# Moving the tiles of a decoder layer to other addresses in SBUF

## The chip, the cores and the metric

The kernel runs on one core of one Trainium2 chip. The metric is the device time of one execution in microseconds. One execution of the kernel before was also profiled; its span, from the first to the last instruction, is a little shorter than the time measured for that execution.

## The reference

One layer of a hybrid decoder on 256 tokens of width 2048, all in float32. A normalised input goes through one wide projection into the queries, keys and values of two attention branches (8 heads of 128 each), 8 forget logits and two gates. The branches are merged through sigmoid gates, projected and added to the input. Then comes an MLP of width 8192 with a squared ReLU, and a last normalisation.

```python
hn = rms_norm(x, norm_mix_g)
z = hn @ w_in                                   # 2048 -> 6*1024 + 8 + 2*2048
a   = merge_heads(moba_attention(...)) @ w_proj_a
bfx = merge_heads(forgetting_attention(...)) @ w_proj_b
merged = sigmoid(g_a) * a + sigmoid(g_b) * bfx
x = x + merged @ w_out                          # 2048 -> 2048
hm = rms_norm(x, norm_mlp_g)
x = x + square(relu(hm @ w_up)) @ w_down        # 2048 -> 8192 -> 2048
out = rms_norm(x, norm_final_g)
```

With 256 tokens there is a single block of MoBA, so that branch is plain causal attention with ALiBi.

## The kernel before

**Weights.** All weights come from HBM in chunks of 1 MB (`load`, line 92), each into one of three `raw` tiles of 128 partitions by 8 KB. Every float32 number is used as a sum of two float32r parts, high and low. ScalarE writes the high part of a piece of a chunk into a slot of the ring `his` (12 slots, line 135, `emit_high`), and VectorE subtracts it from the chunk and writes the low part into the ring `los` (10 slots, line 150, `emit_low`). A slot has 512 float32 columns, which are 2 KB in each partition. A chunk of kind "W" also has four sums of its blocks in the tile `sum` (lines 162 to 164), which are split in the same way: with them a product of 2x2 blocks takes seven multiplications in place of eight.

**Activations.** The factors of a large product (the transposed input, and blocks and sums of blocks of it) are split in the same way and lie in the one tile `big`, 2 x 52 factors of 128 columns (512 bytes) each. The tiles named `pr` (pool `pair`, nine buffers of 4 KB) hold split activations of the plain products, head pairs, merged rows and MLP rows. `row` tiles (three of 8 KB) hold results of a group of columns, `tmp` tiles (five of 2 KB) short-lived rows.

**Products.** Every large product is the function `triple` (line 326): three matmuls into one PSUM bank, high x high, high x low, low x high. The factor is the stationary operand (128 x 128), the split weight the moving one (512 columns; 256 in one short stretch at the end). There are 5604 of these matmuls, nearly all of TensorE's work. Between them stand small blocks into the bank `aux`: transposes (lines 684, 644, 753: moving operand `ident`), scores and values of attention (609, 610, 658, 659) and the forget logits (537, 539).

**Order.** The order on every engine is fixed in the program. `pump` issues splits as slots of the rings come free, `boundary` puts small tasks between pieces of the large products. The DMA of chunk q+3 is issued on SP's queue when VectorE has finished with chunk q. ScalarE's queue issues six DMAs; GpSimd issues none.

**Addresses.** A tile's address in its partition follows from the order of allocation. At the start of SBUF lies a reserve for dynamic DMAs (16 KB by default), then four small constants, and then the pools in turn: `const` (with `his`, `los` and small tables), `big`, `pair`, `rows`, `wraw`, `work`. Whatever is added at the front shifts all that follows.

Of the kernel before, what the change touches and what calls it, by code (L numbers as in the profile page):

```python
# [7 lines left out]
FT = mybir.dt.float32  # L8
# [54 lines left out]
def hybrid_layer(ctx: ExitStack, tc, x, xt, gcols, w_in, w_f, b_forget, w_proj_a, w_proj_b, w_out,  # L63
                 w_up, w_down, norm_final_g, out):
    nc = tc.nc
    const = ctx.enter_context(tc.tile_pool(name="const", bufs=1))
# [10 lines left out]
    chunks = []  # L77
    raw = {}
    split = {}
    his = const.tile([128, HI_SLOTS, 512], FR, name="his")  # L80
    los = const.tile([128, LO_SLOTS, 512], FR, name="los")

# [615 lines left out]
            del state["qk", h]  # L698


    acc2 = const.tile([128, NT, 4], FT, name="acc2")
    inv2 = const.tile([128, NT], FT, name="inv2")
    acc3 = const.tile([128, NT, 5], FT, name="acc3")
# [286 lines left out]
```

## Time and profile before

| | |
|---|---|
| time, median of 3 runs (lowest, highest) | 1362.66 us (1362.04, 1363.45) |
| the profiled execution, its own time | 1362.37 us |
| its span | 1360.7 us |
| TensorE matmul busy | 1342.2 us (99%) |
| TensorE weight load busy | 1108.5 us (81%) |
| VectorE busy | 1076.9 us (79%) |
| ScalarE busy | 797.4 us (59%) |
| GpSimd busy | 20.3 us (1%) |
| DMA engines, mean rate | 193 GB/s |

The matmuls overlap in the pipeline, so a matmul's listed duration is longer than its distance to the next one; the distance between two starts is what a matmul costs in a row of them. A span of many matmuls divided by their number gives it directly. Weight loads lie beside the matmuls. The other engines are bounds only in a stretch where they are busy nearly all the time.

### The profile page before, as it was taken

What the parts mean: (1) busy time and instruction counts of PE and PEld (TensorE: products, weight loads), DVE (VectorE), ACT (ScalarE), POOL (GpSimd) and SP (SyncE); (2) the same over time, 40 slices, a digit from 0 to 9 for tenths busy, and PEclk for the clock granted to TensorE, in tenths of its full rate; (3) what the DMA queues carried; (4) which work ended last, traced back from release to release, by engine and by line L of the source; (5) the groups of instructions that cost most, each with busy time, mean ns of one, the idle gap of its engine ahead of it and who ended that gap; (6) DMA issues with size and microseconds to landing.
All of it is one profiled execution on the core that took longest, in us unless ns stands there. A gap on an engine that the chain in (4) does not pass through costs nothing.

```text
span 1360.7 us, 16488 instructions
## 1 busy us (share of the span) xinstructions
PE 1342.2 (99%) x6132; PEld 1108.5 (81%) x6132; DVE 1076.9 (79%) x1319; ACT 797.4 (59%) x1033; POOL 20.3 (1%) x29
## 2 busy tenths in 40 slices
PE   9999999999999999999999999999999999999997
PEld 7778888877788888888788888888888888888886
DVE  5789999999977996666899557995579955799664
ACT  6766677766664565555566544665446653467532
POOL 0000000012100000000000000000000000000000
PEclk9999999999999999999999999999999999999999
DMA  8555555445465566564466654565645665556661
GB/s 311 186 185 187 186 186 186 157 155 184 160 211 186 188 211 222 175 243 169 157 216 223 205 189 165 189 234 188 201 168 186 221 212 186 183 188 216 225 203 69
DMA packets 93824, 262.25 MB, mean 193 GB/s; under 512 B 4656, under 2 KB 5040, under 8 KB 93104
## 3 DMA queue, kind: packets, MB, share of 16 engines
q1 hardware_dynamic: 92752, 257.97, 55.4%
q10 hardware_dynamic: 992, 3.24, 0.6%
q8 instruction: 48, 0.79, 0.2%
q14 instruction: 32, 0.26, 0.1%
HBM read 259.09 MB, written 2.10 MB: 192 GB/s over the span
## 4 chain that ended last, share of the span: by engine, by line
PE 89%; DVE 6%; ACT 3%; issue 1%; DMA 1%; POOL 0%; SPq 0%; POOLq 0%; ACTq 0%; DVEq 0%
PE P L326 85%; DVE los L150 2%; PE aux L684 2%; DMA raw<-in_w_in_dram 1%; ACT his L135 1%; DVE sum L162 1%; DVE sum L163 0%; PE aux L658 0%; PE aux L610 0%; PE aux L644 0%; ACT row L713 0%; ACT pr L460 0%; ACT big L418 0%; ACT row L486 0%; PE aux L753 0%
## 5 line engine op out<-in xcount | busy, mean ns | idle before, releaser
L326 PE MATMUL P<-his,big 128*128 128x512 f32 x2152 | 693.3, 396 | 0.5 <-ACT row L392 0.5
L135 ACT ACTIVATE his<-raw 128x1024 fp32r<-128x1024 f32 (+1 forms) x494 | 474.4, 970 | 361.9 <-PE P L326 347.6
L150 DVE TENSOR_TENSOR los<-raw,his 128x1024 fp32r<-128x1024 f32 (+1 forms) x511 | 537.3, 1080 | 141.2 <-PE P L326 99.4
L326 PE MATMUL P<-his,pr 128*128 128x512 f32 (+1 forms) x1584 | 491.1, 388 | 1.8 <-ACT his L501 1.8
L326 PEld LDWEIGHTS P<-his,big 128*128 128x128 f32 x2152 | 405.3, 188 | 85.8 <-ACT row L392 1.3
L326 PE MATMUL P<-los,big 128*128 128x512 f32 x1076 | 420.1, 390 | 0.0
L326 PEld LDWEIGHTS P<-his,pr 128*128 128x128 f32 x1584 | 295.9, 188 | 60.8 <-ACT his L501 2.1
L326 PE MATMUL P<-los,pr 128*128 128x512 f32 (+1 forms) x792 | 305.7, 386 | 0.0
L326 PEld LDWEIGHTS P<-los,big 128*128 128x128 f32 x1076 | 203.0, 189 | 40.1
L150 DVE TENSOR_TENSOR los<-sum,his 128x1024 fp32r<-128x1024 f32 (+1 forms) x158 | 163.9, 1073 | 12.2 <-PE P L326 11.0
L326 PEld LDWEIGHTS P<-los,pr 128*128 128x128 f32 x792 | 149.1, 188 | 29.2 <-DVE los L502 0.4
L135 ACT ACTIVATE his<-sum 128x1024 fp32r<-128x1024 f32 (+1 forms) x148 | 142.8, 982 | 31.6 <-PE P L326 18.9
L162 DVE TENSOR_TENSOR sum<-raw 128x1024 f32<-128x1024 f32 x68 | 82.9, 1220 | 0.9 <-DMA raw<-in_w_in_dram 0.9
L164 DVE TENSOR_TENSOR sum<-sum,raw 128x512 f32<-128x512 f32 x68 | 47.5, 698 | 2.3
L163 DVE TENSOR_TENSOR sum<-sum,raw 128x512 f32<-128x512 f32 x68 | 47.5, 698 | 2.3
L772 DVE TENSOR_TENSOR pr<-tmp,pr 128x512 fp32r<-128x512 f32 x32 | 22.0, 689 | 30.0 <-ACT pr L771 30.0
L684 PEld LDWEIGHTS aux<-ident,row 128*128 128x128 f32 x224 | 27.9, 142 | 9.1 <-DVE cumT L591 1.3
L684 PE MATMUL aux<-ident,row 128*128 128x128 f32 x224 | 33.6, 272 | 1.2 <-DVE cumT L591 0.9
L769 ACT ACTIVATE tmp<-aux 128x512 f32<-128x512 f32 x32 | 19.1, 598 | 26.2 <-PE aux L684 26.1
L407 DVE TENSOR_TENSOR big<-pr,big 128x384 fp32r<-128x384 f32 (+1 forms) x16 | 10.0, 624 | 23.4 <-ACT big L406 23.4
L631 ACT ACTIVATE tmp<-tmp,stat 128x128 f32<-128x128 f32 (+1 forms) x32 | 14.3, 447 | 16.9 <-DVE stat L623 16.8
L776 DVE SCALAR_TENSOR_TENSOR row<-P,inv,row 128x512 f32<-128x512 f32 x24 | 17.1, 749 | 8.9 <-PE P L326 8.9
(138 smaller groups left out, 513.4 us busy)
## 6 DMA issues: line engine op xcount, KB each, us to landing
raw<-in_w_in_dram SPq DMA_DIRECT2D x79, 1024.0 KB, 5.3
raw<-in_w_up_dram SPq DMA_DIRECT2D x64, 1024.0 KB, 5.0
raw<-in_w_down_dram SPq DMA_DIRECT2D x64, 1024.0 KB, 5.2
raw<-in_w_out_dram SPq DMA_DIRECT2D x16, 1024.0 KB, 5.1
raw<-in_w_proj_a_dram SPq DMA_DIRECT2D x8, 1024.0 KB, 5.2
raw<-in_w_proj_b_dram SPq DMA_DIRECT2D x8, 1024.0 KB, 5.2
row<-in_xt_dram SPq DMA_DIRECT2D x8, 256.0 KB, 8.3
row<-in_x_dram SPq DMA_DIRECT2D x2, 1024.0 KB, 7.5
```

The costliest lines, as they stand in the source:

```text
L135: nc.scalar.activation(his[:, s:s + m], src[:, j:j + m], AF.Copy)
L150: nc.vector.tensor_tensor(los[:, s + jj:s + jj + mm], src[:, j + jj:j + jj + mm], his[:, h:h + mm].bitcast(FT), OP.subtract)
L162: nc.vector.tensor_tensor(t[:, 0:2], r[:, 1:3], r[:, 0:1].to_broadcast([128, 2, 512]), OP.add)
L163: nc.vector.tensor_tensor(t[:, 2], t[:, 0], r[:, 2], OP.add)
L164: nc.vector.tensor_tensor(t[:, 3], t[:, 2], r[:, 3], OP.add)
L326: nc.tensor.matmul(p, l, r[:, :n], start=first and j == 0, stop=last and j == 2)
L407: nc.vector.tensor_tensor(fa[:, 1, o + i:o + 4], f[:, i:4], fa[:, 0, o + i:o + 4].bitcast(FT), OP.subtract)
L631: nc.scalar.activation(t[:, sl], t[:, sl], AF.Exp, bias=st[:, tok:tok + 1], accum_out=st[:, 2 + tok:3 + tok])
L684: nc.tensor.transpose(p[:, c, s * 128:(s + 1) * 128], src[:, tok, (i + c) * 128:(i + c + 1) * 128], ident)
L769: nc.scalar.activation(t, p, AF.Square)
L772: nc.vector.tensor_tensor(h[:, :, 1], t, h[:, :, 0].bitcast(FT), OP.subtract)
L776: nc.vector.scalar_tensor_tensor(t, p, inv2[:, tok:tok + 1], t, op0=OP.mult, op1=OP.add)
```

## The change

The reserve for dynamic DMAs is set to 1 KB, and two unused tiles of 960 bytes are allocated: one ahead of `his`, one ahead of the last small tables of the pool `const`. No instruction is added, removed or moved on any engine, and no wait differs: only line numbers and addresses do.

```diff
+    const.tile([128, 240], FT, name="pad")
     his = const.tile([128, HI_SLOTS, 512], FR, name="his")
     los = const.tile([128, LO_SLOTS, 512], FR, name="los")
...
+    const.tile([128, 240], FT, name="pad2")
     acc2 = const.tile([128, NT, 4], FT, name="acc2")
...
-    nc = _bacc.Bacc("TRN2", target_bir_lowering=False, num_devices=1)
+    nc = _bacc.Bacc("TRN2", target_bir_lowering=False, num_devices=1, dynamic_dma_scratch_size=1024)
```

In the two programs as built, the addresses in bytes from the start of a partition are:

| tile | before | mod 2048 | mod 128 | after | mod 2048 | mod 128 |
|---|---|---|---|---|---|---|
| `his` (moving operand) | 16512 | 128 | 0 | 2112 | 64 | 64 |
| `los` (moving operand) | 41088 | 128 | 0 | 26688 | 64 | 64 |
| `ident` (moving operand of transposes) | 61792 | 352 | 96 | 47392 | 288 | 32 |
| `big` (stationary operand) | 68736 | 1152 | 0 | 55296 | 0 | 0 |
| `pr`, first of nine (stationary operand) | 121984 | 1152 | 0 | 108544 | 0 | 0 |
| `row`, first of three | 158848 | 1152 | 0 | 145408 | 0 | 0 |
| `raw`, first of three (written by DMA) | 183424 | 1152 | 0 | 169984 | 0 | 0 |
| `tmp`, first of five | 208000 | 1152 | 0 | 194560 | 0 | 0 |
| `sum` | 218240 | 1152 | 0 | 204800 | 0 | 0 |

Since slots are 2 KB and factors 512 bytes long, before the change the moving and the stationary operand of every large matmul begin at the same place within 512 bytes (128); after it the moving operand begins 64 bytes after the place of the stationary one.

## Rows read from the trace of the kernel before

**Rows 1.** The page: busy time of each engine, and slices of DVE.

```profile
PE 1342.2 (99%) x6132; PEld 1108.5 (81%) x6132; DVE 1076.9 (79%) x1319; ACT 797.4 (59%) x1033; POOL 20.3 (1%) x29
...
DVE  5789999999977996666899557995579955799664
```

**Rows 2.** Chain that ended last, longest pieces: start us, us, what.

```profile
381.58 162.62 PE P L326 x717
...
763.54 119.05 PE P L326 x525
```

**Rows 3.** Busy time by stretch: stretch, its length, each engine, PEclk, DMA share, GB/s.

```profile
70.00:140.00 70.00, 68.77 (x313) 55.99 (x312) 62.84 (x71) 47.23 (x59) 0.00 (x0) 0.98 0.56 190
140.00:270.00 130.00, 129.12 (x610) 106.99 (x609) 125.54 (x178) 92.19 (x144) 0.00 (x0) 1.00 0.51 175
270.00:420.00 150.00, 148.27 (x668) 119.18 (x667) 133.06 (x187) 98.17 (x157) 14.90 (x8) 1.00 0.54 183
420.00:700.00 280.00, 278.89 (x1261) 230.76 (x1260) 220.71 (x261) 159.31 (x203) 0.00 (x0) 1.00 0.58 197
...
71.00:72.30 1.30, 1.30 (x4) 0.99 (x3) 0.30 (x1) 1.30 (x2) 0.00 (x0) 0.50 0.41 63
```

**Rows 4.** The same for line 326 alone (PE, PEld, clock, DMA, GB/s).

```profile
270.00:420.00 150.00, 137.53 (x568) 104.80 (x567) 1.00 0.54 183
420.00:700.00 280.00, 275.62 (x1197) 223.35 (x1196) 1.00 0.58 197
700.00:1000.00 300.00, 296.92 (x1291) 240.91 (x1290) 1.00 0.58 198
1000.00:1360.00 360.00, 349.24 (x1566) 285.99 (x1564) 1.00 0.55 187
```

**Rows 5.** Timeline of TensorE while half the clock was granted: start us, us, what.

```profile
71.09 0.63 PE L326 MATMUL P<-los,big 128*128 128x512 f32 x1
71.52 1.05 PE L326 MATMUL P<-his,big 128*128 128x512 f32 x2
72.37 0.63 PE L326 MATMUL P<-los,big 128*128 128x512 f32 x1
```

**Rows 6.** Chain from 380 us: float32 matmuls of 256 columns, two records each.

```profile
380.27 0.43 PE aux L658 x2
```

**Rows 7.** Groups of TensorE's matmuls: line, operands, shapes, count, busy us, mean ns.

```profile
L684 PE MATMUL aux<-ident,row 128*128 128x128 f32 x224 | 33.6, 272 | 1.2 <-DVE cumT L591 0.9 <-ACT cum L583 0.4
...
L609 PE MATMUL aux<-pr 128*128 128x128 f32 x32 | 6.2, 275 | 0.9 <-ACT tmp L646 0.9
```

**Rows 8.** Groups of VectorE, then of ScalarE, same columns.

```profile
L150 DVE TENSOR_TENSOR los<-raw,his 128x1024 fp32r<-128x1024 f32 x377 | 457.2, 1221 | 137.4 <-PE P L326 96.4 <-issue 21.8 <-ACT his L135 16.4
...
L150 DVE TENSOR_TENSOR los<-raw,his 128x512 fp32r<-128x512 f32 x134 | 87.9, 685 | 3.7 <-PE P L326 3.0 <-ACT his L135 0.4
...
L163 DVE TENSOR_TENSOR sum<-sum,raw 128x512 f32<-128x512 f32 x68 | 47.5, 698 | 2.3
L135 ACT ACTIVATE his<-raw 128x1024 fp32r<-128x1024 f32 x394 | 414.0, 1057 | 332.7 <-PE P L326 323.7 <-DMA raw<-in_w_in_dram 2.2 <-DMA raw<-in_w_out_dram 2.0
...
L135 ACT ACTIVATE his<-raw 128x512 fp32r<-128x512 f32 x100 | 62.0, 626 | 29.2 <-PE P L326 24.0 <-DMA raw<-in_w_in_dram 3.5 <-DMA raw<-in_w_up_dram 1.7
```

**Rows 9.** DMA: queues by kind, and waits of SP's queue (us, times, longest).

```profile
q1 hardware_dynamic: 92752, 257.97, 55.4%
q10 hardware_dynamic: 992, 3.24, 0.6%
...
SPq L92 <- DVE los L150: 1142.6, 228, 15.5
```

**Rows 10.** Chain at the program's start: start us, us, what.

```profile
1.72 5.04 DMA raw<-in_w_in_dram
...
7.14 9.54 DMA raw<-in_w_in_dram
```

## The prediction

> **What bounds the kernel now.** I read the page's busy times first, then the chain of waits, then the table by stretch, then the distance between matmuls. TensorE is busy 99% of the span [rows 1], and the chain of waits runs through line 326 in pieces of hundreds of matmuls without another engine between them [rows 2]. So the time is the number of matmuls times the distance between two of them, and the question is whether addresses set that distance. 162.62 us over 717 matmuls are 226.8 ns, and 119.05 over 525, the first of three such pieces, are 226.8 again [rows 2]. These pieces use all slots of `his` and `los` and both `big` and `pr`.
>
> 512 columns at the granted 2.4 GHz are 213.3 ns, so each matmul has 13.5 ns on top. While half the clock was granted, as from 71.0 to 72.3 us [rows 3], the starts stand at 71.09, 71.52 and, two matmuls later, 72.37 us [rows 5]: three matmuls in 1.28 us, 426.7 ns each, which is 512 columns at 1.2 GHz with nothing on top. So the 13.5 ns belong to something that the slower array hides: the supply of operands, or a fixed pause between two matmuls. This is the only thing that I see on the path that an address could change. Float32 matmuls of 256 columns, each in two records, take 0.43 us for two records, 215 ns each [rows 6]: the same 213.3 ns of array time with only 2 ns on top. There columns are taken at half the rate, so again there is slack in the supply.
>
> VectorE is the second bound, and only early: 125.54 of 130 us between 140 and 270 us, 133.06 of 150 after that, 220.71 of 280 from 420 on [rows 3], as its row of slices also shows [rows 1]. The DMA queue is no bound: SP's queue stood 1142.6 us waiting for VectorE to give a `raw` tile back [rows 9].
>
> **The change part by part.** No instruction, order or wait differs. All that can change is how long something takes.
>
> *Moving operands, from 0 to 64 bytes past a multiple of 128.* 5508 matmuls of 512 columns (the 5604 of line 326 less 96 of 256) begin elsewhere. Every large matmul before has the same place within 128 bytes, so no row shows line 326 at another one; it has to be bounded. From below: the 215 ns of the float32 pair [rows 6] against 226.8, a gain of 11.8 ns on each. From above: an operand that straddles its boundaries differently could cost up to one more piece of 64 bytes; 64 bytes are 16 columns, at 213.3/512 = 0.417 ns a column 6.7 ns. The nearest rows on a start off a multiple of 128 are transposes: their moving operand `ident` begins 96 bytes past one, and they last 272 ns, against 275 ns for matmuls of the same 128 columns whose moving operand `pr` begins at a multiple [rows 7]. The odd start costs nothing there (though at float32's half rate, where there is slack). I take 0, as those rows say, and keep -11.8 and +6.7 ns for the range.
>
> *Stationary operands, from 128 to 0 past a multiple of 512.* Before the change these begin at four places within 2 KB (128, 640, 1152, 1664), of which the last straddles a 2 KB boundary and the others don't. The clean pieces of the chain go through all four, and pieces with `big` (most of the 717) and with `pr` (most of the 525) average the same 226.8 ns [rows 2]. I take 0; both ends are those of the moving operand, since the two are supplied to the same matmul.
>
> *VectorE's and ScalarE's operands.* `his` is written by ScalarE and read by VectorE, `los` written by VectorE. A subtraction of 1024 columns takes 1221 ns, of 512 columns 685 [rows 8]: 512 more columns cost 536 ns. On ScalarE it is 1057 and 626, 431 ns [rows 8]. Both are steady rates, with TensorE and DMA reading and writing SBUF beside them at every relative position. If the position of two streams mattered, these durations would scatter. I take 0. The largest difference between rows of equal shape is 698 against 685 ns [rows 8]; 13 ns on the some 436 VectorE operations between 70 and 420 us (71 + 178 + 187 [rows 3]) would be 5.7 us either way, at 90% occupancy some 5 us of time.
>
> *DMA targets, from 128 past a multiple of 256 to multiples of 2 KB.* Only the first chunks stand on the path: 5.04 and 9.54 us of the chain at the start [rows 10]; later chunks are there before they are wanted [rows 9]. If these 14.6 us changed by the 13/685 of VectorE's scatter it would be 0.3 us either way; I take 0.
>
> The Trainium skill says more here ("DMA: Bandwidth & Descriptors", How a descriptor splits into AXI transactions): a descriptor that doesn't begin at a multiple of 256 bytes pays for the bytes back to the boundary below. By an estimate from that page's beats, 128 in place of 132 for 4 KB, the 14.6 us would lose 0.4, and the sum would be 1361.9. No row before the change shows an aligned target.
>
> *The reserve.* All data goes through queues of the kind "hardware_dynamic" on SP and ScalarE; no DMA is issued by GpSimd [rows 9]. I take 0. If a reserve of one sixteenth held up the hardware queues, the 1 MB loads would come late, and this would show as waits for DMA, of which ScalarE's groups now name 2 to 4 us each [rows 8].
>
> The sum is 0: 1362.4 us against the profiled execution (1362.37, its span of 1360.7 plus 1.7 around it), which lies 0.3 us under the median of the three runs.
>
> **The rivals.**
>
> *A: nothing changes*, 1362.4 us. For it: VectorE's and ScalarE's steady rates at all relative positions, the four places of the stationary operand, the transposes. Against it: only that no large matmul has yet run with its two operands apart within 512 bytes.
>
> *B: the two streams collide, and the shift parts them.* Each matmul reads 2 KB of moving columns while the next 512 bytes of stationary columns are read. Both start at the same place within 512 bytes today, and the 13.5 ns vanish when the array slows [rows 5], as they would if reads collided. Against it: the overlap of many fixed pauses would look the same. If all of it went, each matmul would take 215 ns: from 420 us on 1197 + 1291 + 1566 [rows 4], less the 96 of 256 columns, are 3958 matmuls, at 11.8 ns 46.7 us. Between 270 and 420 us VectorE has 17 us free, so 568 matmuls [rows 4] could give 6.7; between 140 and 270 only 4.5 us are free and I count 2; before that VectorE and ScalarE lead and I count nothing. 55 us in all, 1307. If half of it went, 1335; a tenth 1357.
> The Trainium skill speaks against this rival ("SBUF — State Buffer", Who interferes with whom): TensorE has one read port for the moving operand and an independent one for the weight load, and waits for no other engine. By that rule B is worth 0 and A holds; no row before the change tells a collision from a fixed pause.
>
> *C: a start at 64 bytes costs the moving stream something.* One more piece of 64 bytes gives 6.7 x 5508 = 37 us: 1399, slower. A quarter of that (16 bytes, 4 columns, 1.7 ns) gives 9.2 us: 1371.6. For it: at full rate the supply is already the limit, so any extra access shows on every matmul, which it need not at half rate. Against it: the transposes [rows 7]. It decides as soon as it costs 0.5 ns a matmul (0.5 x 5508 = 2.8 us, 0.2%).
>
> *D: the smaller reserve limits the queues.* Then chunks come late. With every one of some 240 chunks late by 0.1 us it is 24 us: 1386.
>
> **How the numbers follow.** A 0.46, B 0.32, C 0.18, D 0.04. A measurement of this kernel can tell 0.2% (2.7 us) from no change. B is nearly always faster by more than that, C nearly always slower; D is half harmless. So faster 0.33, same 0.47, slower 0.20. A's own range is 1359.7 to 1365.1. For 8 in 10 I reach into B down to 1322, some three quarters of its full gain, which leaves out about a quarter of B, and into C up to 1380, half of its full cost, which leaves out nearly half of C and half of D. The forecast is that of A, 1362.4 us.
>
> **What would show each step.** The pieces of the chain divided by their count: 226.8 ns again under A, toward 215 under B, 228.5 to 233.5 under C. The half-clock stretch stays at 427 ns in any case. Line 150 at 1221 and 685 ns, line 135 at 1057 and 626, the first two DMA pieces at 5.0 and 9.5 us. Under B, the waits of TensorE for VectorE between 140 and 420 us grow; under D, waits of ScalarE and VectorE for DMA. I am wrong if the distance in a clean piece moves by more than 0.5 ns.

## The result and the profile after

The changed kernel takes 1370.07 us (median of 3 runs, 1369.8 to 1370.72) against 1362.66: a ratio of 1.0054, 95% interval 1.004 to 1.0068, so it is slower by some 7.4 us. The profiled execution has a span of 1368.1 us.

The chain that ended last after the change, longest pieces (start us, us, what); line 328 is line 326 of before:

```profile
381.74 164.14 PE P L328 x717
674.38 38.46 PE P L328 x168
722.15 34.34 PE P L328 x150
766.49 120.18 PE P L328 x525
940.33 120.18 PE P L328 x525
1114.16 120.17 PE P L328 x525
1287.98 67.64 PE P L328 x324
```

The same pieces with the same counts stand there as in [rows 2], each about 1% longer: 164.14 us over 717 matmuls are 228.9 ns in place of 226.8, and 120.18 over 525 are 228.9 too. In these pieces, where no other engine stands between, a large matmul costs some 2.2 ns more.

Busy time by stretch, all engines, after (stretch, length, PE, PEld, DVE, ACT, POOL, clock, DMA share, GB/s), and then TensorE's line 328 alone:

```profile
70.00:140.00 70.00, 67.45 (x312) 54.99 (x311) 62.62 (x71) 46.93 (x59) 0.00 (x0) 1.00 0.56 191
140.00:270.00 130.00, 129.38 (x610) 106.96 (x609) 125.50 (x178) 91.94 (x144) 0.00 (x0) 1.00 0.51 175
270.00:420.00 150.00, 148.49 (x666) 118.92 (x665) 132.47 (x186) 97.82 (x157) 14.88 (x8) 1.00 0.54 182
420.00:700.00 280.00, 278.94 (x1252) 229.08 (x1252) 218.93 (x259) 159.01 (x203) 0.00 (x0) 1.00 0.57 195
```

```profile
420.00:700.00 280.00, 275.67 (x1188) 221.72 (x1188) 1.00 0.57 195
700.00:1000.00 300.00, 296.92 (x1282) 239.18 (x1281) 1.00 0.58 197
```

Between 140 and 270 us, where VectorE was busy for 125.5 of 130 us before and after, TensorE starts the same 610 matmuls as in [rows 3]: VectorE sets the pace there, and slower matmuls cost nothing. From 420 to 700 us the same stretch holds 1188 matmuls of line 328 in place of 1197 [rows 4], from 700 to 1000 it holds 1282 in place of 1291. Followed by number, the matmul that started at 340 us before starts only 0.1 us later after, and the last one 7.5 us later. The half-clock stretch of before at 71 us [rows 3] has no counterpart after (granted clock 1.00 in place of 0.98): there the same matmul starts 1.2 us earlier than before, but at 140 us the two traces are within 0.1 us of each other again, so this is no part of the 7.4 us.

VectorE and ScalarE after (line, operands, shapes, count, busy us, mean ns):

```profile
L152 DVE TENSOR_TENSOR los<-raw,his 128x1024 fp32r<-128x1024 f32 x377 | 457.0, 1220 | 140.4 <-PE P L328 96.4 <-issue 23.8 <-ACT his L137 17.3
...
L152 DVE TENSOR_TENSOR los<-raw,his 128x512 fp32r<-128x512 f32 x134 | 87.8, 684 | 3.4 <-PE P L328 2.6 <-ACT his L137 0.4
```

```profile
L137 ACT ACTIVATE his<-raw 128x1024 fp32r<-128x1024 f32 x394 | 414.5, 1058 | 336.1 <-PE P L328 303.5 <-DVE row L383 22.5 <-DMA raw<-in_w_in_dram 3.3
...
L137 ACT ACTIVATE his<-raw 128x512 fp32r<-128x512 f32 x100 | 61.8, 625 | 31.7 <-PE P L328 23.7 <-DMA raw<-in_w_up_dram 4.3 <-DMA raw<-in_w_in_dram 3.7
```

These are [rows 8] within 1 ns: the splits on VectorE and ScalarE take as long at the new addresses. The two first DMA pieces of the chain, which answer to [rows 10]:

```profile
1.72 5.29 DMA raw<-in_w_in_dram
7.39 8.95 DMA raw<-in_w_in_dram
```

One is longer and one shorter, 14.2 us together against 14.6.

### The profile page after: what moved, and what is told of

Its sections match the earlier page's. It is cut to its first block, busy times and chain, and to the rows that moved or that the text cites. A ratio compares the mean times of both kernels' runs of the same rounds, so it can differ in the third digit from the quotient of the medians.

```text
span 1368.1 us, 16488 instructions
## 1 busy us (share of the span) xinstructions
PE 1348.4 (99%) x6132; PEld 1107.1 (81%) x6132; DVE 1076.9 (79%) x1319; ACT 797.7 (58%) x1033; POOL 20.3 (1%) x29
## 4 chain that ended last, share of the span: by engine, by line
PE 89%; DVE 5%; ACT 3%; issue 1%; DMA 1%; POOL 0%; SPq 0%; POOLq 0%; ACTq 0%; DVEq 0%
PE P L328 86%; DVE los L152 2%; PE aux L686 2%; DMA raw<-in_w_in_dram 1%; ACT his L137 1%; DVE sum L164 1%; PE aux L612 0%; PE aux L660 0%; DVE sum L165 0%; PE aux L646 0%; ACT row L716 0%; ACT big L420 0%; ACT pr L462 0%; ACT row L488 0%; PE aux L756 0%
## 5 line engine op out<-in xcount | busy, mean ns | idle before, releaser
L633 ACT ACTIVATE tmp<-tmp,stat 128x128 f32<-128x128 f32 (+1 forms) x32 | 14.2, 446 | 16.6 <-DVE stat L625 16.6
```

Of the source, the lines that this page charges most:

```text
L633: nc.scalar.activation(t[:, sl], t[:, sl], AF.Exp, bias=st[:, tok:tok + 1], accum_out=st[:, 2 + tok:3 + tok])
```

## The experiments

Below, "place" is where the moving operand begins past the stationary one, within 512 bytes (and later within 256). Before the change it is 0, after it 64. Distances between matmuls come from the clean pieces of 525 in the chain. Where the three distances inside a triple are told apart, they are means over the recorded starts, from the 13th matmul after a gap on; after the change these are 231.1 ns (first to second matmul), 226.4 (second to third) and 229.2 (third to next), before it 226.8, 226.7 and 226.6.

**The parts of the change.** Four kernels, each from the kernel before.

```diff
 e1: moving operand alone
+    const.tile([128, 16], FT, name="pad")      # ahead of his: 64 bytes
+    const.tile([128, 496], FT, name="pad2")    # ahead of acc2: 1984 bytes
 e2: all but the moving operand
+    const.tile([128, 224], FT, name="pad2")    # ahead of acc2: 896 bytes
 e3: the reserve alone
+    ... num_devices=1, dynamic_dma_scratch_size=1024)
 e4: everything by 64 bytes
+    const.tile([128, 16], FT, name="pad")      # ahead of his
```

> Only his and los (the moving operand of the large matmuls) are shifted, from 128 to 192 past a multiple of 512, so that they begin 64 bytes past a multiple of 128; big, pr and all pools behind keep their places modulo 2 KB, and the reserve stays at 16 KB. Theory M (the start of the moving operand decides): the clean piece of 717 matmuls goes from 226.8 to 228.9 ns each and the time to 1370, as after the whole change. Theory R (the relative place of the two operands decides, 64 bytes apart as after the change): the same. Theory S (the place of the stationary operand, or of the buffers that DMA writes, decides): 226.8 ns and 1362.7.

Measured: 1370.42 us, ratio 1.006 (1.0048 to 1.0073), the same as the whole change; a clean piece of 525:

```profile
766.95 120.18 PE P L327 x525
```

228.9 ns. Theories M and R hold, S falls.

> his and los stay where they were (128 past a multiple of 2 KB); big, pr, row, raw, tmp and sum move to multiples of 2 KB, as after the change; the reserve stays at 16 KB. Theory M (the start of the moving operand within 128 bytes): 226.8 ns a matmul, 1362.7. Theory R (the relative place of the two operands, here 128 bytes apart within 512 in place of 0): something other than 226.8 ns, if not only the 64 counts. Theory S (the place of the stationary operand or of the DMA's targets): 228.9 ns, 1370.

Measured: 1387.77 us, ratio 1.0185 (1.0171 to 1.0199), and in the chain:

```profile
774.96 122.49 PE P L326 x525
951.84 122.00 PE P L326 x525
```

232.4 to 233.3 ns a matmul, although no moving operand moved. M falls: a stationary operand 128 bytes elsewhere costs more than the whole change does. S, which asked for 228.9, falls again. This run is the change without its shift of the moving operand, so the two shifts don't add up: the stationary one alone costs 5.6 to 6.5 ns a matmul, and the moving one on top of it takes 3.5 to 4.4 ns back.

> The reserve alone is 1 KB and no tile is added; every tile moves by 15360 bytes, so that all starts keep their places within 1 KB (moving and stationary operand both at 128 past a multiple of 512). Theories M, R and S: 226.8 ns a matmul and 1362.7. The rival that the smaller reserve holds up the DMA queues: 226.8 ns in clean pieces, but waits for DMA and a time toward 1370.

Measured: 1362.45 us, ratio 0.9998 (0.9989 to 1.0007). The reserve costs nothing.

> 64 bytes are added ahead of his, and everything behind moves by 64 bytes with it: moving and stationary operand both begin at 192 past a multiple of 512, so 64 past a multiple of 128, but at the same place relative to each other as before. Theory M (the absolute start of the moving operand): 228.9 ns a matmul, about 1370. Theory R (the relative place): 226.8 ns, 1362.7. Theory S: unlike the kernel before too, since the stationary operand is off a multiple of 128.

Measured: 1362.89 us, ratio 1.0 (0.9991 to 1.0009), and the clean piece is that of before:

```profile
764.33 119.05 PE P L327 x525
```

Both operands begin 64 bytes past a multiple of 128, as the moving one does after the change, and it is free. So the absolute start costs nothing; the relative place is what counts (theory R).

**The map of places.** Only the length of one pad ahead of `acc2` differs, from the kernel before; the moving operand stays.

```diff
+    const.tile([128, (512 - place) // 4], FT, name="pad2")
```

> The reserve is 16 KB; his and los stay; big, pr and all pools behind move by 64 bytes, so that the moving operand begins 64 bytes BEFORE the stationary one within 512 bytes (448 past it). Theory P (what counts is how far the two are apart, either way): 228.9 ns a matmul in clean pieces and 1370, as with 64 after. Theory Q (the order counts: it costs when the moving operand lies past the stationary one): 226.7 ns or less, 1362.8 or faster. Theory 128 (a difference that is no multiple of 128 is what costs): 228.9.

> As the run before with 128 bytes: the moving operand begins 384 past the stationary one within 512 (128 before it). Theory P: 232.7 ns and 1388, as with 128 after. Theory Q: 226.7 ns or less.

> As before with 256 bytes: the two operands are 256 apart within 512, as far as they can be. Theory P, rising with the distance: over 232.7 ns, some 237, and about 1405. If the pattern repeats every 256 bytes: 226.7 ns and 1362.8.

> As before; the moving operand begins 192 bytes past the stationary one within 512. Theory P, rising with the distance: between the runs with 128 (232.7 ns) and with 256. If the pattern repeats every 256 bytes: as with 448 (64 before).

> The moving operand begins 32 bytes past the stationary one (within 256), his and los where they were. If 0 is the best place and the cost rises from there (0, 64, 128, 192 past gave 226.7, 228.9, 232.7, 233.3 ns a matmul): between 226.7 and 228.9, and 1363 to 1370. If the best place lies between the multiples of 64: under 226.7 and a time under 1362.

> The moving operand begins 32 bytes before the stationary one (224 past it within 256). If 0 is the best place and the cost falls to it steadily from 192: some 230 ns and 1376. If only the piece of 64 bytes that a start falls into counts: as 192, 233.3 ns and 1391, and the run with 32 as 0. If the best lies between: under 226.7 ns.

> The moving operand begins 96 bytes past the stationary one within 256, between 64 (228.9 ns a matmul) and 128 (232.7). If the cost is low around 64 and full elsewhere, as 32 and 128 say: 231 to 233.3 ns and 1380 to 1391. If 64 is one end of a second good stretch: 228.9 or less.

Measured, in the order of the place within 256 bytes:

| place mod 256 | run (place in 512) | piece of 525, us | ns a matmul | time, us | ratio (95% interval) |
|---|---|---|---|---|---|
| 0 | before (0) | 119.05 | 226.8 | 1362.66 | |
| 0 | e7 (256) | 119.06 | 226.8 | 1362.93 | 0.9999 (0.9989 to 1.0008) |
| 32 | e9 (32) | 122.50 | 233.3 | 1391.1 | 1.0206 (1.019 to 1.0221) |
| 64 | after (64) | 120.18 | 228.9 | 1370.07 | 1.0054 (1.004 to 1.0068) |
| 96 | e16 (96) | 122.49 | 233.3 | 1391.97 | 1.0212 (1.0183 to 1.0242) |
| 128 | e6 (384) | 122.01 | 232.4 | 1387.81 | 1.0182 (1.0165 to 1.0199) |
| 192 | e8 (192) | 122.51 | 233.4 | 1390.92 | 1.0206 (1.019 to 1.0221) |
| 192 | e5 (448) | 122.51 | 233.4 | 1391.04 | 1.0208 (1.0192 to 1.0223) |
| 224 | e10 (480) | 122.49 | 233.3 | 1390.62 | 1.0205 (1.0188 to 1.0222) |

The clean pieces of three of them, one chain after another:

```profile
763.32 119.06 PE P L326 x525
```

```profile
776.69 122.51 PE P L326 x525
```

```profile
777.13 122.50 PE P L326 x525
```

These are places 256, 192 and 32. The pairs of places that are 256 apart agree (0 and 256, 192 and 448, and within 1 ns 128 in e2 and 384), so the pattern repeats every 256 bytes. It doesn't rise with the distance (theory P falls: 32 apart costs as much as 192), and it doesn't ask which operand lies ahead (Q falls). Theory 128 falls too: 128 apart, which it held to be free, costs 5.6 ns. For 32 both expectations missed; for 224 the value of 192 was met, but 32 was not free as the same thought asked; 96 was met by its first case. There is one good place, 0; the common price elsewhere is 6.6 ns (233.3 less 226.7), which is 16 columns at 213.3/512 = 0.417 ns; and 64 pays a third of it, 128 a little less than all. Places 160 and those that are no multiple of 32 were not tried. No place tried is better than that of the kernel before.

A wrong place costs nothing while half the clock is granted. In e8 (place 192) the clock is 0.50 from 69.7 to 72.9 us:

```profile
70.70 0.63 PE L326 MATMUL P<-los,big 128*128 128x512 f32 x1
71.13 1.05 PE L326 MATMUL P<-his,big 128*128 128x512 f32 x2
71.98 0.63 PE L326 MATMUL P<-los,big 128*128 128x512 f32 x1
```

Three matmuls in 1.28 us are 426.7 ns each, the same as before the change [rows 5]. Half-clock stretches of e5, e6, e10 and e16 (places 192, 128, 224 and 96) have 426 to 427 ns from start to start too. So the price of a wrong place is there only at full clock, like the 13.5 ns on top of 213.3.

**One operand of three.** Which matmul pays?

```diff
 e11: low parts of the factors in big 128 bytes on (high parts, pr, his, los stay)
-    xT = big.tile([128, 2, SIZE, 128], FR, name="big")
+    xT = Apart(big.tile([128, 2 * SIZE * 128 + 128], FR, name="big"))
...  # Apart gives [:, 0] from element 0 and [:, 1] from SIZE * 128 + 32; x1T in the same way
 e12: los 128 bytes on (his, big, pr stay)
+    const.tile([128, 32], FT, name="padm")     # between his and los
+    const.tile([128, 96], FT, name="pad2")     # ahead of acc2
```

> Of the factors in big only the low parts (stationary operand of the third matmul of a triple) move by 128 bytes; high parts, pr, his and los stay. Theory N (the load of the NEXT matmul's weights runs beside the moving columns of the present one and gets in their way): in the products with big the distance from the second to the third matmul grows toward 232.7 ns, the others stay near 226.7. Theory O (a matmul's own weights): the distance from the third to the next grows instead. In products with pr nothing changes.

Measured: 1372.46 us. In products with `big` the distances are 226.7, 232.5 and 234.2 ns, with `pr` 226.6, 226.7 and 226.8. The distance from the second to the third matmul grows, as theory N said, but so does the one from the third to the next, as O said. So the misplaced weights cost beside the matmul ahead of them and beside the one that uses them as well; the next distance is back at 226.7. As only one operand of TensorE has moved here, and every other tile has kept its place within 256 bytes, it is TensorE's own two operands that count, not one of them against another engine's.

> Only los (moving operand of the second matmul of a triple) moves by 128 bytes; his and the stationary operands stay. If each matmul's cost is set by its own moving operand against the weights that are loaded beside it: the distance from the second to the third matmul is some 232.7 ns, the two others 226.7, and the time is about a third of the way to 1388, 1371. If the lag carries over from one matmul to the next: all three distances change, and the time is not a third of the way.

Measured: 1389.59 us, and distances of 235.6, 233.9 and 230.1 ns. Though one moving operand of three is misplaced, all three distances grow, and the time is that of a place wrong for all. "Each by itself" falls; the reading that is left of the two is that a lag carries over from one matmul to the next.

**One operand that doesn't walk.** Single runs, read by their clean pieces.

```diff
 e13, e15 (e15 with place 192):
-            nc.tensor.matmul(p, l, r[:, :n], ...)
+            nc.tensor.matmul(p, l[:, :1].to_broadcast([128, 128]), r[:, :n], ...)
 e14:
+            nc.tensor.matmul(p, l, r[:, :1].to_broadcast([128, n]), ...)
 e17:
+            m = 64 if j == 1 else 128
+            nc.tensor.matmul(p[:m], l[:, :m], r[:, :n], ...)
```

> Left out: in the large products all columns of the moving operand are the first column of the split weight, read again and again from one address. Places as before. Theory L: the moving operand no longer walks through SBUF, so it doesn't meet the weight load in the same way, and the distance is not 226.7 ns; if a repeated column needs no new read, some 216. Theory F: 226.7 ns.

Measured: 1313.92 us; chain:

```profile
376.80 155.14 PE P L326 x717
742.50 113.70 PE P L326 x525
```

216.4 and 216.6 ns, three above 512 columns at 2.4 GHz. So the 13.5 ns of the kernel before are no fixed pause between matmuls (theory F falls): 10 of them go when the moving operand is read from one address. This was run at place 0 alone; whether a wrong place still costs then was not tried.

> Left out: in the large products all 128 columns of the stationary operand are the factor's first column, read 128 times from one address, so what is computed is not the layer. Places as before the change. Theory L (the 13.4 ns over 213.3 are reads of the next weights that run along 256-byte steps beside the moving columns and hold them up): with the weights read from one address the distance in clean pieces is no longer 226.7 ns, and may go to some 216. Theory F (the 13.4 ns are a fixed pause between two matmuls at full clock, and places only lengthen it): 226.7 ns still.

> The same as the run with one stationary column (what is left out is the same), with the moving operand 192 bytes past the stationary one within 256, where the whole load gave 233.3 ns. Theory L: the same distance as the run with one stationary column at place 0, since nothing walks in step. If the start addresses alone count: 233.3 against 226.7 as before.

Measured: 1376.11 and 1382.37 us. The clean pieces of e13 wander, those of e15 don't:

```profile
770.90 121.35 PE P L326 x525
945.99 120.17 PE P L326 x525
1120.24 120.18 PE P L326 x525
```

```profile
772.76 121.62 PE P L326 x525
948.60 121.62 PE P L326 x525
```

228.9 to 231.1 and 231.7 ns. Weights from one address don't make the matmuls faster; at place 0 they are slower than before, and most of the difference between places 0 and 192 goes (231.7 less 228.9 to 231.1, in place of 6.6). Theory L's 216 is not reached, and the two runs are near each other, not equal.

> Left out: the second matmul of every triple (high factor by low weight) has 64 of its 128 stationary columns, so half of that product's rows lack it. Places as before the change. Theory L (the load of the next weights holds up the moving columns beside it): the distance from the first to the second matmul, beside which half as much is loaded, falls from 226.7 toward 220 ns; the two others stay at 226.7. If a matmul's own weights count: the distance from the second to the third falls instead. Theory F (a fixed pause): all three 226.7.

Measured: 1375.08 us; distances 228.9, 230.5 and 230.0 ns, none of them shorter than before:

```profile
769.55 120.64 PE P L327 x525
```

Half the load beside one matmul of three makes all three slower. L in this form falls: it is not the amount that is loaded. It may be that the good place gives a regular rhythm of two equal streams, which loading less breaks; no run shows this.

**The cost undone inside the change.** e18 is the changed kernel with a second pad of 256 elements in place of 240, so that `big` and all behind lie 64 bytes further on, at place 0 again.

```diff
-    const.tile([128, 240], FT, name="pad2")
+    const.tile([128, 256], FT, name="pad2")
```

> The changed kernel, except that the second pad is 64 bytes longer: big, pr and all behind begin 64 bytes past a multiple of 2 KB, and so do his and los. If the relative place within 256 bytes is the whole cost of the change: 226.7 ns a matmul in clean pieces and 1362.8, although the reserve is 1 KB and both operands are off a multiple of 128. If anything else of the change costs: above 1364.

Measured: 1362.69 us, ratio to the kernel before 0.9999 (0.9989 to 1.0008), with

```profile
764.31 119.06 PE P L328 x525
```

226.8 ns. 64 bytes undo the whole loss, with the small reserve and odd starts still there.

## Why the prediction was wrong

The time lies in the stated range, but the forecast was "no change" and the kernel is slower by 7.4 us. The step that failed is the pricing of TensorE's two operands, each by itself and each at 0: the runs show that their difference modulo 256 sets the price, 2.2 ns a matmul at the 64 bytes of the change. Point by point:

- *What bounds the kernel* was right: TensorE's distance between matmuls times their number, with VectorE in front up to some 340 us. It was also right that what lies on top of 213.3 ns was the one thing on the path that an address could change, and that most of it, 10 of 13.5 ns, belongs to the supply of operands (e14). The half-clock stretch stayed at 427 ns, as it said, wherever a kept trace has such a stretch without gaps, at wrong places too.
- *Moving operands: "I take 0".* This is the first half of the step that failed. A moving operand 64 bytes past a multiple of 128 with nothing else changed (e1) measured +2.2 ns, as the whole change did, within the bounds of -11.8 and +6.7. From 380 us on, some 3500 matmuls of clean stretches went from 226.7 to 228.9 ns on average: 7.7 us. The some 500 within 12 of a gap were about as slow before (229.4) as after (229.0) and give back 0.2. That is the whole loss. The value was read from transposes [rows 7], which take columns at half the rate and have slack; the text said so and took them all the same. By the addresses built, the two operands of those transposes lie at place 224 before and 32 after, two places that cost a large matmul 6.6 ns, and their mean listed duration is 272 ns before and 273 after: at half the rate the place doesn't show. A row at another rate was no evidence for a stream that already waits for its supply.
- *Stationary operands: "I take 0"* is the other half. It rested on four places that are all alike within 256 bytes, and the moving operand stood at the same place beside each, so on one case. e2 prices this shift by itself at 25 us; that the whole change costs only 7.4 is because the shift of the moving operand takes most of it back.
- *VectorE and ScalarE* were right (1220 and 684, 1058 and 625 ns), but the conclusion drawn from them was not: that their durations don't scatter says nothing on TensorE's own two operands.
- *DMA targets* cost nothing to be seen: 14.2 against 14.6 us at the start, and 15.2 in e18 whose targets are off again, so that is scatter. By the estimate from the Trainium skill's rule in "DMA: Bandwidth & Descriptors" (How a descriptor splits into AXI transactions) 0.4 us were to be gained; the scatter is larger than that, so these runs neither bear it out nor speak against it.
- *The reserve* is free (e3), and rival D falls.
- *Rival B* looked at the right thing, the two streams seen relative to each other, with the wrong sign: it took equal places for the collision, and they are the best ones tried. *Rival C* had the right sign, but not the reason: a start at 64 is free when both operands have it (e4, e18). That its lower case (9.2 us, 1371.6) is near the result is luck: it took 1.7 ns where 2.2 were measured, and counted all 5508 matmuls where only those from some 340 us on lengthen the time. Its full price of 6.7 ns is that of most wrong places (6.6 measured), also by luck, since the piece of 64 bytes that it came from is shown by no run; for the whole kernel it is 28 us (1391), and not 37, for the same reason of counting.
- The Trainium skill ("SBUF — State Buffer", Who interferes with whom) gives TensorE two independent read ports and lets it wait for nobody. For other engines the trace agrees: with VectorE busy for 219.98 of the 300 us from 700 on and the DMA engines at 0.58, 3458 of the 3471 settled distances of before, from 380 us on, are 226 or 227 ns. For its two operands the runs don't: the measurement decides, and their relative place moves a matmul by up to 6.6 ns.

Why the relative place of the two operands counts stays open. Shown are the period of 256 bytes, that the price is there only at full clock (e8), that 10 of the 13.5 ns at place 0 go when the moving operand doesn't walk (e14), that one misplaced operand lengthens distances beyond that of its own matmul (e11, e12), and that loading less does not help (e17).

## What to carry to other kernels

Where float32r matmuls like these (128 x 128 by 512 columns, at full clock) follow each other without a gap, look at the addresses of the two operands modulo 256: equal was best of the places tried, and 32 bytes apart cost 2%. Other types and shapes were not tried. Tiles added ahead of others, even unused or small ones, can move that place, so an unexplained change of 1 or 2% after an unrelated edit is worth a look at the built addresses, and a pad of the right length takes it back. Price an address from rows at the same rate, or say that no row bears on it.

## What the runs showed of the hardware that was not expected

- 512 columns of float32r at the granted 2.4 GHz take 226.8 ns from start to start at the best place tried, 13.5 more than half of the 426.7 that they take at 1.2 GHz; one repeated column takes 216.5.
- The relative place of the two operands counts modulo 256 bytes: 226.8 ns at 0, 228.9 at 64, 232.4 at 128, 233.3 at 32, 96, 192 and 224.
- The common price is 16 columns' time a matmul, and one misplaced operand of three (`los` in e12) costs as much as all. At half the clock it is 0 (426.7 ns at places 0 and 192).
